# A bidirectional encoder block in float32: common rows for x and the first weights, seven products for SwiGLU's first pair, sums of weights made in DRAM, and a halved last tile

## The chip, the core and the metric

The kernel runs on one core of a Trainium2 chip. The metric is the device time of one execution in microseconds (us), median of several runs. TensorE (PE in the profile) multiplies; VectorE (DVE), ScalarE (ACT) and GpSimd (POOL) do the rest; SyncE (SP), POOL and ACT issue transfers (DMA).

## The reference, cut to what matters

x has 512 tokens of 1024 features; all is float32.

```python
h = rmsnorm(x, g_mix);  proj = h @ w_in            # 1024 x 11264
xc, gb, gc, q, k, v, g_sw, gate_a, gate_r = split(proj)
y_a = (gb * conv3(gc * xc)) @ w_a_out
y_r = (groupnorm(retention(rotary(q), rotary(k), v)) * g_ret * silu(g_sw)) @ w_r_out
x = x + (sigmoid(gate_a) * y_a + sigmoid(gate_r) * y_r) @ w_o
h2 = rmsnorm(x, g_ffn)
x = x + (silu(h2 @ w_ff_gate) * (h2 @ w_ff_up)) @ w_ff_down      # 2816 wide
y = rmsnorm(x, g_final)
```

## The kernel before

**Arithmetic.** Each float32 operand is split into a high part (rounded to fp32r) and a low part (the rest), and each product is three matmuls: high x high, high x low, low x high. `split` (L170 to L180) makes a high part on ScalarE (L173) and a low part on VectorE (L174). Weights are split on the chip too, in units of 128 x 1024.

**Seven products instead of eight.** Most pairs of weight matrices are treated as a 2 x 2 block matrix b11, b12, b21, b22 (for SwiGLU: gate and up are the two block columns, the halves of the features the two block rows), and the activations as a11 ... a22 by halves of tokens and features. Strassen's scheme in Winograd's form needs seven products, with sums of activations (s1 to s4, `sums`, L588) and sums of weights: t1 = b11 + b12, t2 = t1 + b22, t3 = b12 + b22, t4 = t2 + b21. `prefetch_form` (L243) makes a sum of weights in place on VectorE (L251), and then splits it. `prod` (L324) is one product for SwiGLU: 24 matmuls of 256 columns. `prod_tm` (L358) is one for the quads of w_in (v with the swish gate, the two branch gates), for w_a_out and for the down projection: 24 matmuls of 512 columns (18 where n is 3).

**The order.** `plan` (L58) lists all units of weights in the order in which they are used. `take` hands out the next one and calls `prefetch` until AHEAD = 2 units are ready; `prefetch` first calls `load_raws`, which issues loads for units up to LEAD = 4 places ahead on SP's queue, into ten raw buffers. The order of instructions on each engine comes from a scheduler that keeps dependencies and goes mostly by program order.

**The start.** x is loaded transposed, in blocks of 128 features; `prefetch(4, ...)` loads x's blocks 0 to 3 and the first block of weights in turns (256 KB, 256 KB, 256 KB, 256 KB, 512 KB, 512 KB), and splits them in turns. WARM = 8 matmuls of ones run while the first data are on their way.

**The middle.** q and k of three heads; six quads (`do_quad`, L656), whose results are stored to DRAM on POOL's queue through nine 128 x 512 tiles; convolution, retention, output projections. The loop over nb (L963) makes the residual stream's four token blocks; `ev_o` normalises each and `tr_o` transposes it.

**SwiGLU.** Eleven pairs of 256 gate and 256 up columns, in parts of 3, 4 and 4, each part followed by its down projection. The first pair (`first_pair`, L1018) takes eight plain products, two of them before the last `tr_o`. `begin(q)` is a11 x b11, `second(q)` a12 x b21, `pair(q)` the other five. `gated` applies silu and makes the activations' sums for the down projection.

**The end.** The last down projection adds into y in SBUF: `to_y` adds a finished 128 x 512 bank and squares it with a sum per row, `rms` makes the reciprocal root, `put` scales and stores. The last product finishes token blocks 0 and 1 of the second half of the columns.

Of the kernel before, what the change touches and what calls it, by code (L numbers as in the profile page):

```python
# [17 lines left out]
P = 128  # L18
# [23 lines left out]
WARM = 8  # L42
# [15 lines left out]
def plan():  # L58
# [68 lines left out]


def loads():
# [11 lines left out]
LOADS = loads()  # L141


@with_exitstack
def block_kernel(ctx: ExitStack, tc: tile.TileContext, xT, xtok, wpack, wquad, cols, decs, rot, g_ffn, g_final, out):
# [59 lines left out]
    def prefetch_block(pieces, loads, splits, inbig):  # L205
# [4 lines left out]
        per = max(1, pieces // 2)  # L210
        m = QH // per
        for c, (o, n) in enumerate(((0, 512), (512, 512), (QH, QH)) if pieces > 2 else ((0, QH), (QH, QH))):
            if loads:
                loads(c)
            nc.sync.dma_start(st[o // QH][:, o % QH:o % QH + n], wpack[i][:, o:o + n])
        for half in range(2):
            hi, lo = unit(inbig)
            units.append((hi, lo))
            for c in range(per):
                sl = slice(c * m, (c + 1) * m)  # L220

                round = None if made else nc.vector.tensor_copy
                made.append(split(st[half][:, sl], hi[:, sl], lo[:, sl], round=round))
                if splits:
                    splits(half * per + c)
        return units

    raws = {}

# [5 lines left out]
    def load_raws(upto):  # L235
        while loaded[0] < len(LOADS) and LOADS[loaded[0]][0] <= upto:
            _, quad, name, u, n = LOADS[loaded[0]]
            t = rawtile()
            nc.sync.dma_start(t[:, 0:n], wquad[loaded[0]][:, 0:n])
# [3 lines left out]
    def prefetch_form(quad, f, u, nk):  # L243
# [3 lines left out]
        here = {"t1": "b11", "t2": "b11", "t4": "b11", "t3": "b12"}.get(f, f)  # L247
        more = {"t1": "b12", "t2": "b22", "t4": "b21", "t3": "b22"}.get(f)
# [7 lines left out]
    def prefetch(pieces=1, loads=None, splits=None):  # L256
# [5 lines left out]
        load_raws(i + LEAD)  # L262
        if x[0] == "c":
            units = prefetch_block(pieces, loads, splits, x[1] == "w_o" and x[2] == 512 and x[4] == 512)
# [93 lines left out]
    def prod_tm(n, lhs, pss, start, stop=False, evict=None, part=None):  # L358

        w = []  # L360
        for u in part or range(0, n, 2):
# [8 lines left out]
            for tt in range(2):  # L370
                for u0, (wh, wl) in units:
                    for k in range(u0, min(u0 + 2, n)):
                        c = slice((k - u0) * 512, (k - u0 + 1) * 512)
                        xh, xl = lhs(k, slice(tt * P, (tt + 1) * P))
                        for i, (l, r) in enumerate(((xh, wh), (xh, wl), (xl, wh))):
                            nc.tensor.matmul(pss[tt], l, r[:, c], start=start and k == 0 and i == 0,  # L376
                                             stop=stop and k == n - 1 and i == 2, skip_group_check=True)
                if evict:
                    evict(tt)
# [57 lines left out]
    def load_x(k, n=1):  # L437
        nc.sync.dma_start(xs[k // 4][:, k % 4:k % 4 + n, :], xT[:, k:k + n, :])

    def split_x(k):  # L440
        split(xs[k // 4][:, k % 4, :], xu[0][k // 4][:, k % 4, :], xu[1][k // 4][:, k % 4, :],
              gmix[:, k:k + 1])
# [4 lines left out]

    def split_next(k):
        with tc.issue_after(made[0].ins):
            split_x(k)  # L450

    prefetch(4, lambda c: load_x(c, 1 + c // 2), split_next)
    prefetch(2, lambda c: load_x(4 + 2 * c, 2), lambda c: split_two(4 + 2 * c))
# [53 lines left out]
    for k in range(8):  # L507

        with tc.issue_after(made[min(k + 1, 3)].ins):
            ss.add(xs[k // 4][:, k % 4, :])  # L510
# [40 lines left out]
    def store(dst, t):  # L551
        nc.gpsimd.dma_start(dst, t)
# [4 lines left out]
    for h in range(EARLY):  # L557
        pss = [bank() for _ in range(4)]
        for kk in range(8):
# [4 lines left out]
            if (h, kk) == (1, 1):  # L564
# [3 lines left out]
                for k in range(8):  # L568
                    xk = xs[k // 4][:, k % 4, :]
                    nc.vector.scalar_tensor_tensor(out=xk, in0=xk, scalar=gmix[:, k:k + 1], in1=rrow,  # L570
# [85 lines left out]
    def do_quad(left, right, func, func_left=None):  # L656
        def ev_sum(dst, o, f):
            def ev(tt, t):
                if f:
                    nc.scalar.activation(t, t, f)  # L660
                store(dst[:, o + tt, :], t)
            return ev

        def ev21(tt, ps):
            t = t512()
            nc.scalar.activation(t, ps, func_left or AF.Copy)
            store(left[:, 2 + tt, :], t)
# [295 lines left out]
    for nb in range(NB):  # L963
# [6 lines left out]
        hs[nb] = ev_o(nb, [po[half][nb] for half in range(2)])  # L970

# [46 lines left out]
    def first_pair():  # L1018
        w = {}
        g0, u0, g1, u1 = bank(), bank(), bank(), bank()  # L1020
        _, (w["b11"],) = take()
        prod(w["b11"], XF[0, 0], g0, True, False)
        _, (w["b21"],) = take()
        prod(w["b21"], XF[1, 0], g0, False)
        tr_o(NB - 1, hs[NB - 1])
        _, (w["b12"],) = take()
        prod(w["b12"], XF[0, 0], u0, True, False)
        _, (w["b22"],) = take()
        prod(w["b22"], XF[1, 0], u0, False)
        gated(0, 0, g0, u0)  # L1030
# [224 lines left out]
```

## Time and profile before

| | |
|---|---|
| three timed runs | 1031.6, 1033.45, 1033.29 us; median 1033.29 |
| the profiled execution | 1033.17 us; span from first to last instruction 1031.4 |
| TensorE busy | 1021.8 us, 5640 matmuls |
| VectorE, ScalarE, POOL busy | 886.6, 529.5, 114.9 us |
| DMA | 175.06 MB, mean 170 GB/s |

Busy is the share of time with an instruction of the engine in flight. Matmuls overlap one another, so a busy TensorE can still run slower than it could; how far apart matmuls start tells that.

### The profile page before, as it was taken

The page shows a single profiled execution, that of the slowest core. Times are in us where ns is not written, and L with a number is a line of the kernel's source. Part 1 is how long each engine was busy: PE and PEld are TensorE (multiplying, and loading weights), DVE is VectorE, ACT ScalarE, POOL GpSimd, SP SyncE. Part 2 cuts the span into 40 slices and gives each one's busy share as a digit, 9 for nine tenths or more (in the row PEclk, how much of TensorE's full clock was granted, in tenths as well). Part 3 has the DMA queues.
Part 4 walks back from the last instruction along what each step waited for, and adds up shares of the span by engine and source line. Part 5 has one row for each costly group of instructions (what it writes and reads, how often), then busy time and mean ns, then how long its engine had stood idle before and what let it go on. Part 6 is the DMA issues. An engine that isn't in the chain of part 4 may idle for free.

```text
span 1031.4 us, 14797 instructions
## 1 busy us (share of the span) xinstructions
PE 1021.8 (99%) x5640; PEld 892.9 (87%) x5640; DVE 886.6 (86%) x1143; ACT 529.5 (51%) x717; POOL 114.9 (11%) x189
## 2 busy tenths in 40 slices
PE   9999999999999999999999999999999999999997
PEld 7888888888888998888888888889988999899985
DVE  7878898979798988697999988579998899889996
ACT  6546655553656455353533235355555565556553
POOL 0030221121112003202011000000002000110011
PEclk9999999999999999999999999999999999999999
DMA  9524376383746657828267625630319332663322
GB/s 345 188 79 171 127 254 203 136 295 113 234 157 216 255 192 262 322 79 314 66 261 286 223 86 184 222 120 4 103 47 278 106 94 71 193 155 103 123 32 92
DMA packets 49399, 175.06 MB, mean 170 GB/s; under 512 B 6512, under 2 KB 6512, under 8 KB 46000
## 3 DMA queue, kind: packets, MB, share of 16 engines
q1 hardware_dynamic: 35584, 129.26, 36.2%
q0 software_dynamic: 13600, 44.84, 13.5%
q8 instruction: 44, 0.72, 0.3%
q14 instruction: 27, 0.22, 0.1%
q10 hardware_dynamic: 144, 0.03, 0.0%
HBM read 135.56 MB, written 38.54 MB: 169 GB/s over the span
## 4 chain that ended last, share of the span: by engine, by line
PE 96%; DVE 2%; DMA 1%; issue 1%; ACT 0%; POOLq 0%; POOL 0%; SPq 0%
PE bank L376 34%; PE bank L332 27%; PE bank L291 11%; PE bank L292 11%; PE bank L293 11%; DMA raw<-wquad 1%; DVE wlo L174 1%; DMA raw<-wpack 0%; PE bank L945 0%; PE bank L896 0%; DVE xform L174 0%; DVE big L174 0%; DVE big L1147 0%; DVE t L998 0%; DVE t L1014 0%
## 5 line engine op out<-in xcount | busy, mean ns | idle before, releaser
L173 ACT CAST whi<-raw 128x1024 fp32r<-128x1024 f32 (+1 forms) x286 | 292.3, 1034 | 288.3 <-PE bank L376 60.6
L174 DVE TENSOR_TENSOR wlo<-raw,whi 128x1024 fp32r<-128x1024 f32 (+1 forms) x287 | 340.2, 1199 | 82.2 <-ACT whi L173 81.1
L332 PE MATMUL bank<-xform,whi 128*128 128x256 f32 x1440 | 260.3, 283 | 0.0
L332 PEld LDWEIGHTS bank<-xform,whi 128*128 128x128 f32 x1440 | 224.8, 192 | 0.7 <-ACT t L383 0.5
L332 PE MATMUL bank<-xform,wlo 128*128 128x256 f32 x720 | 203.7, 283 | 0.0
L376 PE MATMUL bank<-whi,big 128*128 128x512 f32 x596 | 187.5, 390 | 0.2 <-ACT t L383 0.2
L251 DVE TENSOR_TENSOR raw<-raw 128x1024 f32<-128x1024 f32 (+1 forms) x132 | 156.9, 1202 | 3.0 <-DMA raw<-wquad 1.8
L332 PEld LDWEIGHTS bank<-xform,wlo 128*128 128x128 f32 x720 | 138.2, 192 | 0.0
L376 PEld LDWEIGHTS bank<-whi,big 128*128 128x128 f32 x596 | 111.7, 188 | 24.3 <-ACT t L383 0.6
L376 PE MATMUL bank<-whi,xform 128*128 128x512 f32 x384 | 121.2, 389 | 0.0
L376 PE MATMUL bank<-wlo,big 128*128 128x512 f32 x298 | 116.0, 389 | 0.0
L291 PE MATMUL bank<-big,whi 128*128 128x512 f32 x224 | 87.7, 393 | 0.9 <-DVE whi L173 0.9
L292 PE MATMUL bank<-big,whi 128*128 128x512 f32 x224 | 87.5, 392 | 0.0
L293 PE MATMUL bank<-big,wlo 128*128 128x512 f32 x224 | 87.4, 392 | 0.0
L383 ACT COPY t<-bank 128x512 f32<-128x512 f32 x102 | 59.2, 585 | 52.4 <-PE bank L376 26.3
L376 PEld LDWEIGHTS bank<-whi,xform 128*128 128x128 f32 x384 | 72.1, 188 | 15.0
L376 PE MATMUL bank<-wlo,xform 128*128 128x512 f32 x192 | 74.8, 390 | 0.4 <-DVE wlo L174 0.4
L291 PE MATMUL bank<-whi,big 128*128 128x512 f32 x176 | 68.9, 392 | 0.0
L292 PE MATMUL bank<-wlo,big 128*128 128x512 f32 x176 | 68.5, 389 | 0.0
L293 PE MATMUL bank<-whi,big 128*128 128x512 f32 x176 | 68.1, 390 | 0.0
L376 PEld LDWEIGHTS bank<-wlo,big 128*128 128x128 f32 x298 | 56.0, 188 | 11.5
L291 PEld LDWEIGHTS bank<-big,whi 128*128 128x128 f32 x224 | 42.5, 190 | 9.9 <-ACT big L176 1.2
(175 smaller groups left out, 1373.2 us busy)
## 6 DMA issues: line engine op xcount, KB each, us to landing
raw<-wquad SPq DMA_DIRECT2D x132, 512.0 KB, 4.7
raw<-wpack SPq DMA_DIRECT2D x51, 512.0 KB, 6.3
z<-t POOLq DMA_DIRECT2D x24, 256.0 KB, 5.3
zform<-z POOLq DMA_DIRECT2D x6, 1024.0 KB, 6.1
v<-t POOLq DMA_DIRECT2D x16, 256.0 KB, 5.0
sg<-t POOLq DMA_DIRECT2D x16, 256.0 KB, 3.1
qh<-t POOLq DMA_DIRECT2D x16, 256.0 KB, 2.7
ql<-t POOLq DMA_DIRECT2D x16, 256.0 KB, 2.8
```

Source lines behind the costliest of these rows:

```text
L173: first = (round or nc.scalar.copy)(hi, src)
L174: nc.vector.tensor_tensor(out=lo, in0=src, in1=hi.bitcast(F32), op=ALU.subtract)
L251: nc.vector.tensor_tensor(out=t, in0=t, in1=raws[quad, more, u][:, 0:n], op=ALU.add)
L291: nc.tensor.matmul(ps, lh, rh, start=first, stop=False)
L292: nc.tensor.matmul(ps, lh, rl, start=False, stop=False)
L293: nc.tensor.matmul(ps, ll, rh, start=False, stop=last)
L332: nc.tensor.matmul(o, l[:, c], r[:, k], start=start and s == 0 and k == 0 and i == 0, stop=stop and k == 3 and i == 2, skip_group_check=True)
L376: nc.tensor.matmul(pss[tt], l, r[:, c], start=start and k == 0 and i == 0, stop=stop and k == n - 1 and i == 2, skip_group_check=True)
L383: nc.scalar.copy(t, ps)
```

## The change

Five parts:

1. x's blocks 0 to 3 and the first block of weights lie in common rows (`xw`): four transfers of 512 KB, each with 512 columns of x and 512 of weights, into four raw buffers. x's scaling by the row norm writes to another tile than it reads. WARM is 10.
2. The first pair uses the seven products. `begin` and `second` of pairs 0 and 1 and `begin` of pair 2 come before the first `pair`; `tr_o` of the last token block and `sums` come after `second(0)`. Two calls of `prefetch` are added in the loop over nb.
3. For pairs 0 and 1 the sums of weights are made in DRAM by 16 transfers on POOL's queue (8 copies, 8 that add), one after some of the stores of each quad; the finished forms are loaded as raw units, without L251.
4. In the last product the second token block is done by halves of its columns (2 x 256), and each half is added and squared on its own.
5. The final norm multiplies the gain by sqrt(D) beforehand (ScalarE) instead of dividing the sum of squares by D; the sum of squares is finished on POOL instead of VectorE; one of the last stores is issued by ScalarE.

```diff
-WARM = 8
+WARM = 10
...
-    f(0, "b11", "b21", "b12", "b22")
+    f(0, "b11", "b21")
     f(1, "b11", "b21")
+    f(2, "b11")
     for q0, n in FF_PARTS:
-        for q in range(max(q0, 1), q0 + n):
+        for q in range(q0, q0 + n):
             f(q, *(x for x in FORMS[1:5] if q > 1 or x != "b21"))
-            if q + 1 < NQ:
+            if 1 < q < NQ - 1:
                 f(q + 1, "b11")
             f(q, "t4", "b22")
...
+SUMMED = (("f", 0), ("f", 1))
...
-            need = name if quad == ("f", 0) else NEEDS.get(name)
+            need = name if quad in SUMMED else NEEDS.get(name)
...
-    return out
+    return out + [(len(PLAN), quad, "b12", 0, 4 * WIDTH[quad[0]]) for quad in SUMMED]
...
+    steps = [(quad, f, g, add) for group in (
+        (("t1", "b11", 0), ("t3", "b22", 0)), (("t1", "b12", 1), ("t3", "b12", 1)),
+        (("t2", "t1", 0),), (("t2", "b22", 1),), (("t4", "t2", 0),), (("t4", "b21", 1),))
+        for quad in SUMMED for f, g, add in group]
+
+    def sum_step(behind=None):
+        if steps:
+            quad, f, g, add = steps.pop(0)
+            src = wsum[quad, g] if g[0] == "t" else quarter(quad, g)
+            with tc.issue_after(behind.ins):
+                if add:
+                    nc.gpsimd.dma_start(out=wsum[quad, f], in_=src, accum_op=ALU.add, max_dma_last_dim=4 * CH)
+                else:
+                    nc.gpsimd.dma_start(wsum[quad, f], src)
...
+    for k in range(4):
+        nc.sync.dma_start(xw_sb[k], xw[k])
+    units = [unit(), unit()]
+    for k in range(4):
+        sl = slice(k % 2 * 512, (k % 2 + 1) * 512)
+        hi, lo = units[k // 2]
+        made.append(split(xw_sb[k][:, 512:], hi[:, sl], lo[:, sl], round=None if k else nc.vector.tensor_copy))
+        with tc.issue_after(made[0].ins):
+            split_x(k)
...
-                store(dst[:, o + tt, :], t)
+                last = store(dst[:, o + tt, :], t)
+                if tt and not o:
+                    sum_step(last)
...
             if tt:
                 turn_one()
+                sum_step(last)
...
         hs[nb] = ev_o(nb, [po[half][nb] for half in range(2)])
+        if nb in (1, 3):
+            prefetch()
...
-    first_pair()
+    begin(0)
+    second(0)
+    tr_o(NB - 1, hs[NB - 1])
+    XF.update(sums(xf32[0, 0], xf32[1, 0], xf32[0, 1], xf32[1, 1]))
     begin(1)
     second(1)
+    begin(2)
     for q0, n in FF_PARTS:
-        for q in range(max(q0, 1), q0 + n):
+        for q in range(q0, q0 + n):
             pair(q)
...
+    nc.scalar.activation(gf, gf, AF.Copy, scale=float(math.isqrt(D)))
...
     def rms(nb):
-        ac = acs[nb]
-        nc.vector.scalar_tensor_tensor(out=ac[:, 5:6], in0=ac[:, 1:2], scalar=1.0 / D,
-                                       in1=ac[:, 4:5], op0=ALU.mult, op1=ALU.add)
+        ac, i = acs[nb], done[nb] - 1
+        nc.gpsimd.tensor_scalar(out=ac[:, 5:6], in0=ac[:, i:i + 1], scalar1=ac[:, 4:5], scalar2=None, op0=ALU.add)
         nc.gpsimd.tensor_tensor(out=ac[:, 7:8], in0=ac[:, 5:6], in1=mhalf[:, 0:1], op=ALU.pow)
...
-            nc.sync.dma_start(out[nb * P:(nb + 1) * P, half * 512:(half + 1) * 512], yt)
+            (nc.scalar if (nb, half) == (1, 0) else nc.sync).dma_start(
+                out[nb * P:(nb + 1) * P, half * 512:(half + 1) * 512], yt)
...
-    prod_tm(n, forms["s4"], d, False, True, lambda tt: ev(d[tt], tt, 1))
+    prod_tm(n, forms["s4"], d, False, True, lambda tt, c: ev(d[tt], tt, 1, c), halves=True)
```

## Rows read from the trace of the kernel before

**Rows 1.** The page, busy us by engine, share of the span, instructions.

```profile
PE 1021.8 (99%) x5640; PEld 892.9 (87%) x5640; DVE 886.6 (86%) x1143; ACT 529.5 (51%) x717; POOL 114.9 (11%) x189
```

**Rows 2.** Waits of TensorE: us in total, times, longest.

```profile
PE bank L291 <- DVE whi L173: 0.9, 1, 0.9
```

**Rows 3.** The chain that ended last: start us, us, what.

```profile
699.31 57.86 PE bank L332 x480
```

**Rows 4.** Stretches: busy us (instructions) by engine, granted clock, DMA share, GB/s.

```profile
4.80:5.70 0.90, 0.03 (x1) 0.01 (x1) 0.55 (x2) 0.07 (x1) 0.00 (x0) 1.00 0.83 280
5.70:9.60 3.90, 3.88 (x9) 3.13 (x10) 2.84 (x6) 2.56 (x5) 0.00 (x0) 1.00 0.99 339
9.60:26.40 16.80, 16.80 (x75) 13.88 (x75) 15.06 (x20) 12.34 (x19) 0.00 (x0) 1.00 1.02 403
75.00:325.00 250.00, 249.63 (x1102) 206.31 (x1101) 216.46 (x234) 146.67 (x187) 41.53 (x77) 1.00 0.55 192
655.00:692.30 37.30, 37.30 (x185) 31.02 (x184) 21.42 (x33) 17.95 (x34) 1.64 (x3) 1.00 0.36 119
692.30:780.40 88.10, 88.10 (x653) 83.81 (x651) 81.44 (x103) 49.88 (x73) 3.31 (x3) 1.00 0.25 79
1028.25:1029.50 1.25, 0.00 (x0) 0.00 (x0) 0.00 (x0) 0.00 (x0) 0.00 (x0) 0.50 1.01 380
```

**Rows 5.** Groups of VectorE by form, 692.3 to 780.4: busy us, mean ns.

```profile
L174 DVE TENSOR_TENSOR wlo<-raw,whi 128x1024 fp32r<-128x1024 f32 x23 | 28.0, 1219 | 0.9 <-ACT whi L173 0.6
L251 DVE TENSOR_TENSOR raw<-raw 128x1024 f32<-128x1024 f32 x14 | 16.8, 1219 | 1.9 <-DMA raw<-wquad 1.8
...
L1014 DVE TENSOR_TENSOR t<-t,t 128x256 f32<-128x256 f32 x9 | 3.5, 418 | 0.0
```

**Rows 6.** POOL's queue, 90 to 130 and 764 to 800: packets, MB, share.

```profile
q0 software_dynamic: 960, 3.15, 20.9%
...
q0 software_dynamic: 1147, 2.09, 34.0%
```

**Rows 7.** Waits of SP's queue: us in total, times, longest.

```profile
SPq L239 <- DVE wlo L174: 519.8, 112, 39.9
```

**Rows 8.** Loads of line L239, 75 to 325.

```profile
DMA to landing us min/median/max: 3.4/4.8/7.5
```

**Rows 9.** Timeline of the start: start us, us, instruction, idle before.

```profile
0.73 0.39 SPq L438 DMA_DIRECT2D big<-xT  x1
...
1.05 3.79 PE L424 MATMUL bank<-ones 128*128 128x128 f32 x16 [1.05 <-DVE lw L609]
...
4.15 0.72 ACT L176 ACTIVATE big<-big,cols_sb 128x512 fp32r<-128x512 f32 x1 [1.40 <-DMA cols_sb<-cols]
...
5.15 0.43 DVE L173 CAST whi<-raw 128x512 fp32r<-128x512 f32 x1 [4.14 <-DMA raw<-wpack]
...
5.72 1.62 PE L291 MATMUL bank<-big,whi 128*128 128x512 f32 x3 [0.89 <-DVE whi L173]
```

**Rows 10.** Loads of x, line L438.

```profile
DMA to landing us min/median/max: 3.2/6.2/9.5
```

**Rows 11.** Timeline of the tail.

```profile
1013.03 0.19 POOL L1126 TENSOR_SCALAR fin<-fin 128x1 f32<-128x1 f32 x1 [8.67 <-ACT t L1124]
...
1024.30 0.69 DVE L1122 TENSOR_TENSOR big<-bank,big 128x512 f32<-128x512 f32 x1 [0.64 <-PE bank L376]
...
1025.03 0.63 ACT L1124 ACTIVATE t<-big 128x512 f32<-128x512 f32 x1 [1.99 <-DVE big L1122]
...
1026.02 0.54 POOL L1135 TENSOR_TENSOR fin<-fin,mhalf 128x1 f32<-128x1 f32 x1 [1.74 <-DVE fin L1133]
...
1026.60 0.75 DVE L1147 SCALAR_TENSOR_TENSOR big<-big,fin,gf 128x512 f32<-128x512 f32 x1 [0.66 <-POOL fin L1135]
1027.38 0.81 SPq L1150 DMA_DIRECT2D y<-big  x2
```

**Rows 12.** A 256-column form on ScalarE, 735 to 745.

```profile
L173 ACT CAST big<-t 128x256 fp32r<-128x256 f32 x1 | 0.4, 402 | 0.0
```

More of the change, by code (lines that the diff above doesn't have):

```diff
@@ L1 @@
+import math
 from contextlib import ExitStack
@@ L203, in unit, with prefetch_block @@
         return hi, lo
-    def prefetch_block(pieces, loads, splits, inbig):
+    def prefetch_block(loads, splits, inbig):
         i = block[0]
@@ L209, in prefetch_block, with quarter @@
         units = []
-        per = max(1, pieces // 2)
-        m = QH // per
-        for c, (o, n) in enumerate(((0, 512), (512, 512), (QH, QH)) if pieces > 2 else ((0, QH), (QH, QH))):
+        for c in range(2):
             if loads:
                 loads(c)
-            nc.sync.dma_start(st[o // QH][:, o % QH:o % QH + n], wpack[i][:, o:o + n])
-        for half in range(2):
+            nc.sync.dma_start(st[c], wpack[i][:, c * QH:(c + 1) * QH])
+        for c in range(2):
             hi, lo = unit(inbig)
             units.append((hi, lo))
[L219 to L225, printed above, removed]
+            split(st[c], hi, lo)
+            if splits:
+                splits(c)
         return units
     raws = {}
+    wsum = {(quad, f): dram.tile([P, QH], F32, name=f"{f}{quad[0]}{quad[1]}")
+            for quad in SUMMED for f in ("t1", "t2", "t3", "t4")}
+    def quarter(quad, name, u=0):
+        return wquad[next(i for i, x in enumerate(QUARTERS) if x[1:4] == (quad, name, u))]
+    steps = [(quad, f, g, add) for group in (
[11 more added lines that the diff above has]
+                    nc.gpsimd.dma_start(wsum[quad, f], src)
     def rawtile():
@@ L238, in load_raws @@
             t = rawtile()
-            nc.sync.dma_start(t[:, 0:n], wquad[loaded[0]][:, 0:n])
+            src = wsum[quad, name] if name[0] == "t" else quarter(quad, name, u)
+            nc.sync.dma_start(t[:, 0:n], src[:, 0:n])
             raws[quad, name, u] = t
@@ L246, in prefetch_form @@
         n = nk * WIDTH[quad[0]]
-        here = {"t1": "b11", "t2": "b11", "t4": "b11", "t3": "b12"}.get(f, f)
-        more = {"t1": "b12", "t2": "b22", "t4": "b21", "t3": "b22"}.get(f)
+        if quad in SUMMED:
+            here, more = f, None
+        else:
+            here = {"t1": "b11", "t2": "b11", "t4": "b11", "t3": "b12"}.get(f, f)
+            more = {"t1": "b12", "t2": "b22", "t4": "b21", "t3": "b22"}.get(f)
         t = raws[quad, here, u][:, 0:n]
@@ L254, in prefetch_form, with prefetch @@
         return [(hi, lo)]
-    def prefetch(pieces=1, loads=None, splits=None):
+    def prefetch(first=False, loads=None, splits=None):
         i = pos[0]
@@ L261, in prefetch @@
         x = PLAN[i]
-        load_raws(i + LEAD)
+        if not first:
+            load_raws(i + LEAD)
         if x[0] == "c":
-            units = prefetch_block(pieces, loads, splits, x[1] == "w_o" and x[2] == 512 and x[4] == 512)
+            units = prefetch_block(loads, splits, x[1] == "w_o" and x[2] == 512 and x[4] == 512)
         else:
@@ L356, in fm_quad, with prod_tm @@
         ev12(u2)
-    def prod_tm(n, lhs, pss, start, stop=False, evict=None, part=None):
+    def prod_tm(n, lhs, pss, start, stop=False, evict=None, part=None, halves=False):
         w = []
@@ L446, in split_two @@
         split_x(k + 1)
[L448 to L453, printed above, removed]
+    prefetch(True, lambda c: load_x(4 + 2 * c), lambda c: split_two(4 + 2 * c))
     rcs = misctile(D, "rcs").rearrange("p (i n) -> p i n", i=2)
@@ L509, in block_kernel @@
         with tc.issue_after(made[min(k + 1, 3)].ins):
-            ss.add(xs[k // 4][:, k % 4, :])
+            ss.add(x_in(k))
     ss.split()
@@ L1172, in block_kernel, with ev @@
     held = []
-    def ev(ps, nb, half):
-        add, square = to_y(ps, nb, half)
+    def ev(ps, nb, half, c):
+        add, square = to_y(ps, nb, half, c)
         if held:
```

104 lines of the change are left out of this document (50 added, 54 removed).

## Prediction

> **What bounds the kernel now.** I read the page first: TensorE is busy 99% of the span [rows 1]. A busy row need not mean full speed, so the waits of TensorE came next: the longest wait of a real matmul is the first one, 0.9 us for the first rounded weights [rows 2]. The chain of waits says at what pace it then runs: 480 matmuls of 256 columns in 57.86 us, 120.5 ns each, one behind the other [rows 3]; the table by stretches gives 75 matmuls of 512 columns in 16.8 us, 224 ns each [rows 4]. So from 5.72 to 1024.3 the time is a count of matmuls, and a change is worth what it does to that count, to the start and to the tail. VectorE is the runner-up: 81.44 of 88.10 us busy in the stretch of the first SwiGLU pairs [rows 4].
>
> The sum is made against the profiled execution: 1033.17 us, span 1031.4 and 1.8 around it. The median of the three timed runs is 1033.29, 0.12 higher; they lie between 1031.6 and 1033.45.
>
> **The change, part by part.**
>
> *One product fewer.* The first pair takes seven products in place of eight. A product is 24 matmuls of 256 columns: 24 x 0.1205 = 2.89 us off the count [rows 3]. This is the surest term, -2.89.
>
> *What feeds it.* The stretch 692.3 to 780.4 holds the first pairs and the start of the first down product. There VectorE loses four sums of weights of pair 1 (4 x 1.22 = 4.88, L251), gains three more splits for pair 0 (3 x 1.22 = 3.66) and three evictions that pair 0 did not have (its b, u3 and u2; 3 x 0.69 = 2.07), and two splits (2.44) move forward by the two added prefetch calls, to 655 to 692.3, where it is busy 21.42 of 37.30 us [rows 4, 5]. That makes 81.44 - 1.59 = 79.85 us of work for a stretch of 88.10 - 2.89 = 85.2 us: 94% instead of 92%. It fits if nothing waits at a bad place. The tightest place is pair 0's s1 and s2: the four sums of activations follow the last transposes as before, but only three products (8.7 us) stand between those and the first use, where eight stood. From the ends far apart (0 if the splits hide, 3.7 us below in the rivals) I take +0.5, near zero, because TensorE's row stays at 88.10 of 88.10 today with VectorE at 92%.
>
> *The sums in DRAM.* Sixteen transfers of 512 KB go on POOL's queue during the six quads: eight copies, eight that add. Nothing on TensorE's path reads them before the first pairs, 300 us later. Price from the queue view: plain stores took 20.9% of 40 us for 3.15 MB, 1.39 us per 512 KB; adding stores 34.0% of 36 us for 2.09 MB, 3.07 us per 512 KB [rows 6]. Together 8 x 1.39 + 8 x 3.07 = 35.7 us of all sixteen DMA engines, over 250 us in which they are 0.55 busy [rows 4]. What hides them: weight loads are sent as soon as a raw buffer is free (SP waited 519.8 us for that, over 112 loads) and land in 4.8 us [rows 7, 8]. I take 0 and keep 35.7 as the far end. Behind each on POOL stand the next stores of the quads, and VectorE and ScalarE wait for the tiles that these free. Pairs 0 and 1 now load seven forms each instead of four blocks; with the DMA engines 0.25 busy there [rows 4], 0. After the last weights two blocks (b12 of both pairs) are loaded that nobody reads: 2 x 1.39 us, some 20 us before SP's last stores; 0.
>
> *The start.* Today x's first block and the first weights are two transfers; the first block alone lands 3.2 us after its issue at 0.73, and the weights let VectorE begin at 5.15 [rows 9, 10]. One transfer of both, issued at 0.73, lands between 3.9 and 5.1; I take 4.6. Then comes ScalarE's 0.72 on x beside VectorE's 0.43 on the weights [rows 9], so data are ready near 5.4. The warm-up grows from 16 rows in 3.79 us to 20, to about 5.8 by the rows' ends, somewhat less by their starts. First real matmul 5.3 to 5.8 instead of 5.72: I take -0.2. Four of the ten raw buffers now hold x until 35 us; the loads that must wait are those that ran far ahead; 0.
>
> *The clock.* In 5.7 to 9.6 nine matmuls took 3.9 us, 433 ns each; from 9.6 on, 224 [rows 4]. That is the spacing of 512 columns at 1.2 and at 2.4 GHz (the column of the granted clock reads 1.00 in both, so here the spacing is what shows it). Before the rise TensorE stood idle 0.9 us between warm-up and first matmul [rows 4]. The longer warm-up closes that gap nearly. What is lost at the lower level is 9 x 0.209 = 1.9 us: the gain lies between 0 (the rise comes at 9.6 as before) and 1.9. I take 1.2: the fastest of the three runs is 1.7 us below the median, about the size of this loss, so executions that lose almost none of it seem to exist. The Trainium skill, TensorE: Matmul & The Clock Gate, "What's actually happening", says that the slow clock is the default and activity releases it; by that rule closing the gap brings the rise forward, and the sum would have 1.9 here, 1028.5 in all (the second rival). Its section "What you observe" calls the moment variable from run to run; no row of this one execution shows that.
>
> *The tail.* From the last add at 1024.30 the chain is: square 0.73 later, rstd by POOL at 1026.02, scale at 1026.60, first store at 1027.38, both stores issued by 1028.19, end at 1031.4 [rows 11]. Now the last half tile is 256 columns: VectorE's 0.69 becomes 0.42 and ScalarE's 0.63 becomes 0.40 [rows 5, 11, 12], 0.50 off. But in the last 2.89 us VectorE has 0.69 + 1.41 + 0.42 + 0.75 = 3.3 us to do (adds and scalings of the tiles before), so the last add starts up to 0.4 late. The sum of squares moves from VectorE to a POOL TENSOR_SCALAR of 0.19 [rows 11]; about nothing. I take -0.3 of 0 to -0.5. Sending one of the two last stores from ScalarE saves half of 0.81 us of issue, 0.4 at most (nothing stands behind it on ScalarE); but while both move, the DMA engines are at 1.01 and 380 GB/s [rows 4], so I take -0.1. The Trainium skill, DMA: Bandwidth & Descriptors, "Issuing engines are not separate DMA queues", says that a second issuing engine saves the issue time only; by that rule the term would be up to -0.4 and the sum 1028.9, by the row of the full engines it is -0.1. The halved matmuls cost 24 x 0.1205 - 12 x 0.224 = +0.20. Tail: -0.2.
>
> *The rest* (gain times sqrt(D) on ScalarE, which is half idle; x's scaling into another tile): 0.
>
> Sum: -2.89 + 0.5 - 0.2 - 1.2 - 0.2 = -4.0. 1033.17 - 4.0 = 1029.2 us.
>
> **The rivals.**
>
> *The clock does not move.* The start brings at most its 0.2, partly spent at the lower level: 1029.2 + 1.2 = 1030.4. For it: nothing in the rows says what the rise asks for; 16 rows of warm-up did not bring it before 9.6. Against: the idle gap was there. Here the change does not do what its longer warm-up would.
>
> *The clock rises with the first real matmul.* All of the 1.9 comes back: 1029.2 - 0.7 = 1028.5. For it: the gap is nearly closed, and the fastest run before. Against: 0.1 to 0.4 us of idle time may stay, and the data of the next blocks must then arrive for 2.7 us (12 x 0.224) each, which 512 KB in 1.4 us do, but VectorE has three operations of 0.69 to 0.75 on each, 2.2 in all.
>
> *VectorE becomes the bound in the first pairs.* If its 6.66 us of idle time in the stretch (88.10 - 81.44) cannot be filled, the stretch takes 79.85 + 6.66 = 86.5 instead of 85.2, and 1.3 comes back; if the two splits are not made early either, 82.3 + 6.66 = 88.95, and 3.7 comes back. Without the 0.5 already counted: 1030.0 to 1032.4, middle 1031.5. For it: 92% busy today. Against: no wait of TensorE there that counts.
>
> *The DRAM sums hold up the stores (slower).* Stores share POOL's queue with the sums. One that lands late keeps its 512-column tile (nine in all); VectorE, in order, stops before the next weight split, and TensorE has only two prepared units of 2.7 us (12 x 0.224). If all of it passed on, 1029.2 + 35.7 = 1064.9. Forecast gains are used up when 11% passes (4.0 of 35.7); it is slower by 0.2% from 17% (6.1); a quarter gives 1038. For it: VectorE 87% busy in 75 to 325 [rows 4] with stores in every quad. Against: each sum is some 3.1 us, and a quad, seven products of 24 matmuls of 0.224, lasts 37.6 and has three.
>
> **How the numbers follow.** A measurement here tells about 0.2% (2.07 us) from no change. Forecast (gap closed, one product fewer, little lost): 0.50, own range 1028.0 to 1030.2. Clock as before: 0.20. Clock up at once: 0.09. VectorE bound: 0.13; its middle, 1031.5, lies within 0.2% of before (above 1031.2). DRAM sums: 0.08. Faster: 0.50 + 0.20 + 0.09 = 0.79; same 0.13; slower 0.08. The range leaves out the DRAM rival, the far end of VectorE's and small tails of the others: 1027.8 to 1031.8.
>
> **What would show it.** Right: matmuls of L332's kind 24 fewer; the first pairs without a wait of TensorE over 0.5 us; the first real matmul near 5.5 and spacings of 224 ns before 9; the adding transfers near 3 us of queue time each and no wait on a store in VectorE's list; the last add 0.42 long. Wrong: a wait of TensorE on an s1 or s2 split near 705, on weight splits in 75 to 325, or 433 ns until 9.6 again. The prediction falls if TensorE's idle time grows by over 2 us anywhere.

## The result

The changed kernel takes 1034.19 us (median of 22 runs, 1032.8 to 1036.36) where the kernel before takes 1032.7 (22 runs, 1031.12 to 1034.77): ratio 1.0016, 95% interval 1.001 to 1.0022. It is slower by 0.16%, within 0.2% of no change; 1029.2 had been forecast, and the range ended at 1031.8. The profiled execution took 1034.5 us, its span is 1032.7, against 1033.17 and 1031.4.

The page of the changed kernel: busy us by engine, share, instructions.

```profile
PE 1020.1 (99%) x5632; PEld 890.8 (86%) x5632; DVE 886.1 (86%) x1142; ACT 536.1 (52%) x726; POOL 125.6 (12%) x210
```

Against [rows 1] TensorE has eight matmuls fewer (24 of the saved product; plus 12 by halving, plus 4 of warm-up) and still the longer span. Where it stands is in its waits, without that of the warm-up: us in total, times, longest.

```profile
...
PE bank L408 <- DVE big L1160: 1.0, 1, 1.0
PE bank L363 <- DVE xform L184: 1.0, 1, 1.0
PE bank L363 <- ACT whi L183: 0.8, 1, 0.8
PE bank L363 <- ACT t L416: 0.5, 1, 0.5
PE bank L322 <- ACT big L186: 0.4, 1, 0.4
PE bank L408 <- DVE big L184: 0.4, 1, 0.4
PE bank L323 <- DMA big<-ql: 0.3, 1, 0.3
```

The kernel before had one wait of 0.9 us that counted [rows 2]. Now L1160, the first line, is the add of a finished bank in the last tile; the three of L363 are in the first SwiGLU pairs; L322 is the first real matmul. The wait on L184 in L363 is the sign that the prediction had named, a wait on a split of s2. The stretches of [rows 4], with the same columns:

```profile
5.70:9.60 3.90, 3.48 (x13) 2.90 (x14) 3.75 (x7) 3.50 (x7) 0.00 (x0) 1.00 1.01 369
...
75.00:325.00 250.00, 250.00 (x1109) 207.16 (x1108) 216.40 (x235) 146.10 (x185) 52.24 (x92) 1.00 0.69 224
655.00:692.30 37.30, 37.30 (x185) 31.07 (x184) 22.42 (x36) 18.21 (x36) 1.64 (x3) 1.00 0.35 121
692.30:780.40 88.10, 85.82 (x623) 80.60 (x622) 81.16 (x103) 54.89 (x78) 2.36 (x3) 1.00 0.34 115
```

Thirteen matmuls lie in the first stretch instead of nine, although the first starts 0.40 us later. The quads, where the sums in DRAM are made (75 to 325), keep TensorE busy all the time. In the first pairs (692.3 to 780.4) it stands idle for 2.28 us.

With matmuls of both kernels laid side by side by their place in the order, the 1.30 us of longer span are: first matmul +0.40; the next ten -1.37; at 82 us -0.70 (a stall of the kernel before is missing); at 520 us +0.63 (the wait for ql); up to the first pairs -0.06; in them -2.89 for the product and +3.53 of waits; from 760 to 785 us -0.34; at 872 us +0.66; last tile and end +1.44.

### The profile page after: what moved, and what is told of

The parts are those of the page before. It is cut to its first block, busy times and chain, and to the rows that moved or that the text cites. A ratio compares the mean times of both kernels' runs of the same rounds, so it can differ in the third digit from the quotient of the medians.

```text
span 1032.7 us, 14838 instructions
## 1 busy us (share of the span) xinstructions
PE 1020.1 (99%) x5632; PEld 890.8 (86%) x5632; DVE 886.1 (86%) x1142; ACT 536.1 (52%) x726; POOL 125.6 (12%) x210
## 4 chain that ended last, share of the span: by engine, by line
PE 68%; issue 17%; DVE 8%; POOL 3%; DMA 2%; ACT 1%; POOLq 0%; SPq 0%; DVEq 0%; ACTq 0%
PE bank L408 31%; PE bank L363 16%; PE bank L322 7%; PE bank L323 7%; PE bank L324 7%; DVE wlo L184 2%; POOL z L597 2%; DVE big L198 1%; DMA big<-ql 1%; DVE big L184 1%; DVE raw L281 1%; DMA z<-t 1%; DMA raw<-wquad 0%; DMA cols_sb<-cols 0%; ACT whi L183 0%
## 5 line engine op out<-in xcount | busy, mean ns | idle before, releaser
L184 DVE TENSOR_TENSOR wlo<-raw,whi 128x1024 fp32r<-128x1024 f32 (+1 forms) x290 | 343.4, 1199 | 87.8 <-ACT whi L183 86.6
L363 PE MATMUL bank<-xform,whi 128*128 128x256 f32 x1424 | 258.2, 284 | 2.3 <-DVE xform L184 1.0
L363 PEld LDWEIGHTS bank<-xform,whi 128*128 128x128 f32 x1424 | 222.2, 192 | 3.9 <-ACT t L416 1.6
L363 PE MATMUL bank<-xform,wlo 128*128 128x256 f32 x712 | 200.8, 283 | 0.0
L408 PE MATMUL bank<-whi,big 128*128 128x512 f32 (+1 forms) x604 | 188.0, 387 | 1.4 <-DVE big L1160 1.0
L281 DVE TENSOR_TENSOR raw<-raw 128x1024 f32<-128x1024 f32 x128 | 152.2, 1202 | 1.7 <-DMA raw<-wquad 0.6
L363 PEld LDWEIGHTS bank<-xform,wlo 128*128 128x128 f32 x712 | 136.3, 192 | 0.0
L408 PE MATMUL bank<-wlo,big 128*128 128x512 f32 (+1 forms) x302 | 116.6, 387 | 0.0
L322 PE MATMUL bank<-big,whi 128*128 128x512 f32 x224 | 87.3, 392 | 0.4 <-ACT big L186 0.4
L322 PE MATMUL bank<-whi,big 128*128 128x512 f32 x176 | 68.9, 392 | 0.0
L323 PE MATMUL bank<-wlo,big 128*128 128x512 f32 x176 | 68.6, 390 | 0.0
L324 PE MATMUL bank<-whi,big 128*128 128x512 f32 x176 | 68.1, 390 | 0.0
L322 PEld LDWEIGHTS bank<-big,whi 128*128 128x128 f32 x224 | 42.3, 189 | 9.4 <-ACT big L186 0.7
```

The costliest lines, as they stand in the source:

```text
L184: nc.vector.tensor_tensor(out=lo, in0=src, in1=hi.bitcast(F32), op=ALU.subtract)
L281: nc.vector.tensor_tensor(out=t, in0=t, in1=raws[quad, more, u][:, 0:n], op=ALU.add)
L322: nc.tensor.matmul(ps, lh, rh, start=first, stop=False)
L323: nc.tensor.matmul(ps, lh, rl, start=False, stop=False)
L324: nc.tensor.matmul(ps, ll, rh, start=False, stop=last)
L363: nc.tensor.matmul(o, l[:, c], r[:, k], start=start and s == 0 and k == 0 and i == 0, stop=stop and k == 3 and i == 2, skip_group_check=True)
```

## The experiments

Each ran in alternation with the kernel before, eleven times or so; ratios are to it, with the 95% interval.

| run | us | ratio |
|---|---|---|
| changed kernel again (c_after) | 1034.05 | 1.0013 (1.0004 to 1.0022) |
| e1_whole | 1032.55 | 0.9998 (0.9989 to 1.0006) |
| e2_two_banks | 1033.12 | 1.0006 (0.9997 to 1.0015) |
| e13_store_sp | 1032.02 | 0.9996 (0.9987 to 1.0005) |
| e7_tail_back | 1031.95 | 0.9993 (0.9984 to 1.0002) |
| e3_sums_first | 1033.68 | 1.0009 (1.0 to 1.0018) |
| e8_pool_s4 | 1034.3 | 1.0014 (1.0005 to 1.0023) |
| e12_order_only | 1034.38 | 1.0019 (1.001 to 1.0028) |
| e6_pe_order | 1031.99 | 0.999 (0.9982 to 0.9999) |
| e4_cols_first | 1033.56 | 1.0011 (1.0002 to 1.0019) |
| e11_before_warm10 | 1031.9 | 0.9996 (0.9988 to 1.0005) |
| e10_no_dram_sums | 1032.12 | 0.9996 (0.9987 to 1.0005) |
| e9_best | 1029.77 | 0.9978 (0.9969 to 0.9987) |

### The last tile and the end

The timeline of the changed kernel's last tile: start us, us, instruction, idle before and its releaser.

```profile
1022.04 1.41 DVE L1186 SCALAR_TENSOR_TENSOR big<-big,fin,gf 128x512 f32<-128x512 f32 x2
...
1022.54 0.28 PE L408 MATMUL bank<-whi,big 128*128 128x256 f32 x1
...
1023.36 0.42 DVE L1160 TENSOR_TENSOR big<-bank,big 128x256 f32<-128x256 f32 x1
...
1023.83 0.39 PE L408 MATMUL bank<-whi,big 128*128 128x256 f32 x1 [1.01 <-DVE big L1160]
...
1027.66 0.75 DVE L1186 SCALAR_TENSOR_TENSOR big<-big,fin,gf 128x512 f32<-128x512 f32 x1 [1.68 <-POOL fin L1174]
```

The first half's last matmul ends at 1022.82. VectorE is at two scalings until 1023.4, adds that half, and only then, 1.29 us after the last start, TensorE begins the second half: other columns, but the same bank. The wait is one for a semaphore that this add raises. Two runs take the wait away in two ways.

```diff
-    prod_tm(n, forms["s4"], d, False, True, lambda tt, c: ev(d[tt], tt, 1, c), halves=True)
+    prod_tm(n, forms["s4"], d, False, True, lambda tt, c: ev(d[tt], tt, 1, c))          # e1_whole
```

> The changed kernel with its last tile whole again (twelve matmuls of 512 columns and one add of 0.69 us, in place of twice twelve of 256 and two adds of 0.42); all else as changed. Theory A (the halves share one PSUM bank; TensorE may not write the second half while VectorE has still to add the first, and VectorE comes to that add late because two scalings of 1.41 us stand before it): the 1.29 us gap at 1022.5 and the 0.17 us that halving costs go, the last add and square are 0.27 and 0.22 longer, so the end is 0.9 to 1.3 us earlier than in the changed kernel, that is 0.3 to 0.7 above the kernel before. Rival B (VectorE is simply behind in the tail, and the gap of TensorE only shows it): the last add stays where it is or later, 0 to 0.4 us gained, 1.2 to 1.6 above before.

```diff
+    d[1] = (d[1], bank())                              # e2_two_banks: columns 256 to 511 in the second
-    prod_tm(n, forms["s1"], d, True)
+    prod_tm(n, forms["s1"], d, True, halves=True)
...
+lambda tt, c: ev(d[1][c.start // 256] if tt else d[0], tt, 1, c), halves=True)
```

> The changed kernel with the last tile's two halves in two PSUM banks (its first product s1 is halved as well, so 12 more matmuls of 512 become 24 of 256, +0.17 us; its add of the tile before becomes two of 256). Theory A (it is the shared bank): the gap of 1.29 us at the start of the last half goes, last add about 1.2 us earlier, net 0.9 to 1.2 us below the changed kernel, 0.4 to 0.7 above before. Rival B (VectorE is behind anyway): the gap goes, but the last add starts less than 0.5 us earlier; 0 to 0.3 gained. Rival C (the wait is not on the bank but on VectorE's queue in some other way): the gap stays.

In both the gap is gone: the spacings from 1015 on are 0.09 and 0.07 us above normal in sum, against 1.33. The timeline with two banks:

```profile
1022.53 0.40 PE L412 MATMUL bank<-whi,big 128*128 128x256 f32 x2
1022.77 0.28 PE L412 MATMUL bank<-wlo,big 128*128 128x256 f32 x1
...
1023.97 0.28 PE L412 MATMUL bank<-whi,big 128*128 128x256 f32 x1
...
1024.28 0.75 DVE L1197 SCALAR_TENSOR_TENSOR big<-big,fin,gf 128x512 f32<-128x512 f32 x1 [0.52 <-POOL fin L1185]
1024.95 0.42 DVE L1164 TENSOR_TENSOR big<-bank,big 128x256 f32<-128x256 f32 x1
```

So the shared bank is the cause of the gap. From the start of the two scalings to the end of the span it is 10.69 us in the changed kernel and 9.70 in e1: 0.99 gained, theory A's size. In e2 it is 10.08. Of the 1.2 us gained there on TensorE only part reaches the end: the last add now waits for a scaling that stands ahead of it on VectorE (1024.28), and from last matmul to ScalarE's last read it is 1.75 us instead of 1.10. In e2 theory A was right on the wait and half of its size; rival B had the other half. The Trainium skill, PSUM — Partial Sum Buffer, "PSUM bank collisions raise a hardware error", says that two engines must not be in one bank (and the same 32 partitions of it) at a time, disjoint columns included, and that programs should guard a bank by semaphores. The trace has such an order (1.29 us from start to start in one bank, 0.12 in two); no run shows what would happen without it.

```diff
-        nc.gpsimd.tensor_scalar(out=ac[:, 5:6], in0=ac[:, i:i + 1], scalar1=ac[:, 4:5], ...)
+        nc.vector.tensor_scalar(out=ac[:, 5:6], in0=ac[:, i:i + 1], scalar1=ac[:, 4:5], ...)   # e7 only
-            (nc.scalar if (nb, half) == (1, 0) else nc.sync).dma_start(
+            nc.sync.dma_start(                                                      # e7 and e13, both with e1
```

> The changed kernel with its whole tail as before: last tile whole, the sum of the two sums of squares on VectorE, all last stores on SP's queue (the gain times the root of D on ScalarE stays). Theory A (three costs: shared bank about 1.2, POOL's sum 0.28 to 0.4, ScalarE's store 0.2): 1.5 to 1.9 us less than the changed kernel, 0.5 to 0.9 less than the run with the whole last tile alone; from ScalarE's read of the last sum of squares to the last scaling 0.85 us, from that to the end 4.8. Rival B (POOL's sum and the store are within the noise of a profile): as the run with the whole last tile alone, within 0.3.

> The changed kernel with its last tile whole and all last stores on SP's queue; the sum of the two sums of squares stays on POOL. Theory A (the store from ScalarE costs some 0.5 us: from the last scaling to the end 5.04 and 5.09 us with it, 4.45 and 4.52 without it in the kernels with the tail as before): last scaling to end 4.4 to 4.6, 0.4 to 0.6 us less than the run with the whole last tile alone. Rival B (what saved it there was VectorE's sum, and the order of the two last scalings): last scaling to end stays at 5.0 or more.

From the end of ScalarE's last read to the last scaling, and from the start of that to the end of the span: before 0.84 and 4.80; changed 1.13 and 5.07; e1 1.08 and 5.07; e13 1.07 and 4.49; e7 0.91 and 4.47. POOL's sum costs 0.2 to 0.3, ScalarE's store 0.6 against the same kernel without it (theory A of e13); e7 is near theory A's 0.85 and beats its 4.8. By the medians it is 2.10 us below the changed kernel (c_after), where its theory A had 1.5 to 1.9. The transfers in the last 20 us, KB each and us to landing, changed kernel and then e13:

```profile
y<-big SPq DMA_DIRECT2D x7, 256.0 KB, 2.1
y<-big ACTq DMA_DIRECT2D x1, 256.0 KB, 2.8
```

```profile
y<-big SPq DMA_DIRECT2D x8, 256.0 KB, 2.0
```

The last landing comes 3.58 us after the last scaling in e1 and 3.48 in e13, so the transfer itself is 0.1 of the 0.6. The rest lies behind the last landing: 1.49 us to the end in e1, 1.00 in e13. There SP waits for the semaphores of the last transfers one after another, in a fixed order; then it drains, and the engines meet. In the kernels with a store from ScalarE SP also pauses for some 0.3 us among these steps; why is open.

The same stretch tells why the kernel before, with both stores on SP as well, needs 4.80 (4.80 to 4.81 in four further profiles). Its last store raises a semaphore that stands early in that order: seven more waits of 0.06 us follow the landing at 1030.07, and SP first drains 0.51 us after it. In e13 one more wait follows the landing at 1028.99, and the drain comes 0.16 us after it. SP's drains in the kernel before, then in e13 (ns, first and last start):

```profile
L1251 SPq DRAIN  x3: 7/7/7, 1030.6 to 1030.9; - x3
```

```profile
L1300 SPq DRAIN  x3: 7/7/7, 1029.1 to 1029.5; - x3
```

### The first pairs

The changed kernel at pair 0's s2 and s3:

```profile
709.56 0.28 PE L363 MATMUL bank<-xform,whi 128*128 128x256 f32 x1
709.58 1.22 DVE L184 TENSOR_TENSOR xform<-big,xform 128x1024 fp32r<-128x1024 f32 x1
...
710.85 0.39 PE L363 MATMUL bank<-xform,whi 128*128 128x256 f32 x1 [1.00 <-DVE xform L184]
...
713.78 1.05 ACT L183 CAST whi<-raw 128x1024 fp32r<-128x1024 f32 x1 [2.10 <-PE bank L363]
...
714.88 0.38 PE L363 MATMUL bank<-xform,whi 128*128 128x256 f32 x1 [0.78 <-ACT whi L183]
...
724.23 1.23 DVE L184 TENSOR_TENSOR wlo<-raw,whi 128x1024 fp32r<-128x1024 f32 x1 [2.86 <-ACT whi L183]
```

TensorE has issued one matmul of s2's high part when the low part is only begun: VectorE, which has no idle time from 695.2 on, is 1.1 us late. The second wait is for a cast that itself waited 2.10 us for TensorE to release a weight buffer: on TensorE some matmuls of pair 1's s1 and s2 stand ahead of pair 0's s3. At 724 VectorE is idle for 2.86 us, so over the whole pair it is not the bound.

```diff
-                ("s1", a22, a21, a22, ...), ("s3", a21, a11, a21, ...),
-                ("s2", a11, a22, a11, ...), ("s4", a12, a12, a11, ...)
+                ("s1", a22, a21, a22, ...), ("s2", a22, a22, a11, ...),     # e3 and e8, second set only
+                ("s3", a21, a11, a21, ...), ("s4", a12, a12, a22, ...)
-            nc.vector.tensor_tensor(out=o, in0=in0, in1=in1, op=op)
+            (nc.gpsimd if s2_next and name == "s4" else nc.vector).tensor_tensor(...)          # e8 only
...
```

(e8 also queues ScalarE's casts of pair 0's weights for s1 and s2 behind its casts of the sums.)

> The changed kernel, with the second set of sums of activations made in the order s1, s2, s3, s4 (s2 overwrites s1's sum, not a11), in place of s1, s3, s2, s4; same operations. Theory A (the stalls of the first pairs come from the order: s2's low part is made by VectorE at 709.6 to 710.8, behind s3's sum and split, 1.0 us after TensorE wants it): s2 is ready 2.4 us or more earlier, the gap at 709.6 (1.16 us above a normal spacing) goes, the kernel gains 0.9 to 1.2 us. Rival B (VectorE is the bound of the stretch; work put off only stalls TensorE later): the gap at 709.6 goes, others of the same sum (at s3, s4 or at the weights of pair 1) take its place, gain below 0.3 us.

> The changed kernel with the second set of sums in the order s1, s2, s3, s4, its s4 sum (128 x 1024, 1.22 us on VectorE) made by POOL, and ScalarE's casts of the weights for pair 0 queued behind the casts of the sums. Theory A (VectorE has no idle time from 695 to 719 and is the bound there; the order alone changed nothing, the same gaps came back to a hundredth): with 1.22 us less to do before s2's low part the gap of 1.28 us at 709.6 goes or falls below 0.3, 0.9 to 1.2 us gained, if POOL's add does not slow VectorE. Rival B (the gap is ScalarE's or TensorE's order, not VectorE's load): gap as before, or moved to s3 with the same sum; nothing gained.

In e3 the same gaps stand at the same distance, 1.28 and 1.06 us. Neither of its theories was met, because the edit did not bring the split forward: ScalarE casts s2 only at 706.95, behind a cast of weights that waits 1.83 us for TensorE to release a buffer, and VectorE takes the split up at 708.80 as before. In e8 the gaps are 1.22 and 1.52, and the reason is new:

```profile
705.68 2.87 POOL L642 TENSOR_TENSOR big<-big 128x1024 f32<-128x1024 f32 x1 [11.58 <-DVE big L642]
...
706.28 5.63 DVE L184 TENSOR_TENSOR xform<-big,xform 128x1024 fp32r<-128x1024 f32 x3
```

The three splits that take 3.49 us in e3 (at 708.80) take 5.63 beside POOL's add: 1.22 us were taken off VectorE and 2.14 put on it. The Trainium skill, SBUF — State Buffer, "Who interferes with whom", says that a VectorE tensor_tensor with both inputs in SBUF contends with POOL's reads; this pair of rows agrees. The run therefore does not tell load from order.

```diff
+        with tc.issue_after(heads_of[0]["s3"].ins) if q == 1 else nullcontext():     # e6 and e12
             _, (w,) = take()
             prod(w, XF["s1"], d, True)
             _, (w,) = take()
             prod(w, XF["s2"], a, False)
         u2 = snap(a)
-        if q > 1:
-            second(q)
+        if q == 0 or q > 2:                                                           # e6 only
+            second(q or 2)
+        elif q == 2:
+            begin(3)
...
```

> The changed kernel with TensorE's order in the first pairs changed: pair 1's first two products are queued behind pair 0's s3 product (in the changed kernel two matmuls of each stand ahead of it), the second product of pair 2's p1 stands between pair 0's s2 and s3, and pair 3's first product between pair 2's s2 and s3. Same products, same work of VectorE. Theory A (the gap of 1.06 us at 713.8 is one of order: a matmul of pair 1 that waits for a weight cast, itself waiting for a weight buffer, stands ahead of pair 0's ready product): that gap goes, 0.6 to 0.9 us gained. Rival B (VectorE has no time left from 695 to 719, and what TensorE does not wait for here it waits for later): the sum of the gaps from 700 to 745 stays at 2.7 us or more, within 0.4.

> The changed kernel with only the order of the matmuls kept: pair 1's first two products behind pair 0's s3 product, without the products of pairs 2 and 3 as cover. Theory A (cover is what was missing: at 709.6 VectorE is 1.1 us late with s2's low part, and TensorE has no product that needs neither that nor the copy of the bank): the gap at 709.6 stays at 1.1 to 1.3, the one at 713.8 becomes a wait of 0.6 to 1.0 for the copy of the bank; 0 to 0.4 us gained. Rival B (the order by itself made the gaps): both gaps go, 1.7 to 2.1 us gained, as with the cover.

(In e6 the list of weights follows the new order.) These two tell it apart. With the order alone (e12) the gap at 708.4 stays at 1.28 and the next grows to 1.78, more than theory A had for it; nothing is gained. The wait is now for the copy of the bank, 1.5 us of the 2.0:

```profile
PE bank L364 <- ACT t L418: 2.0, 2, 1.5
```

With a product of pair 2 as cover (e6) both gaps are gone, though VectorE does the same work as late as before. Between the first matmul of s2's high part (708.64) and the first that waits for its low part (709.93), TensorE now starts nine matmuls of another product (708.76 to 709.73). Sum of spacings above normal from 700 to 736: before 0.34, changed 3.83, e12 4.30, e6 1.48. The longest waits of e6:

```profile
...
PE bank L413 <- DVE big L1168: 1.0, 1, 1.0
PE bank L326 <- DMA big<-ql: 0.5, 1, 0.5
PE bank L367 <- ACT t L421: 0.5, 1, 0.5
...
```

L367 (L363 in the changed kernel) keeps only the wait for pair 1's copy. What was missing was a product that needs neither s2 nor the copied bank, at the moment when VectorE was late. e6 is 2.06 us below the changed kernel in the same series; its theory A had only one of the two gaps going, for 0.6 to 0.9. Cover without the new order was not run.

### The start and the clock

c_after is the changed kernel with no edit; e4 has one line changed; e11 is the kernel before with one.

```diff
-    nc.scalar.dma_start(cols_sb, cols)
+    nc.sync.dma_start(cols_sb, cols)          # e4_cols_first
...
-WARM = 8
+WARM = 10                                     # e11_before_warm10, in the kernel before
```

> The changed kernel again, unchanged, as the measure for the other three on the same chip. Both theories: 1.0 to 2.3 us above the kernel before. Of the start, theory A (the first run's late first matmul, 6.13, was one execution's late landing of the columns) says 5.4 here, as in three of the four runs since; rival B (the common rows make it late) says 6.0 or later.

> The changed kernel with the 28 KB of columns (g_mix among them) issued as the first transfer of SP's queue, ahead of the common rows of x and weights, not on ScalarE's queue beside them. Theory A (ScalarE's first split of x waits for the columns, which share the DMA engines with four transfers of 512 KB and land 4.6 us after their issue): the columns land by about 4.0, the first split of x starts when the first common row lands (4.6 to 5.2), the first real matmul comes 0.3 to 0.6 us earlier than 6.13, and the end with it. Rival B (the row is no earlier than the columns, and is now issued later): the first real matmul at 6.0 to 6.3, nothing gained.

> The kernel before with the warm-up of ten products in place of eight, nothing else. Theory A (the longer warm-up alone brings the full clock to the first real matmuls: a run of the changed kernel with the first real matmul at 5.96, after a gap of 1.24 us, has 0.23 us per 512 columns at once): first real matmul at 5.7 to 5.8, spacing 0.23 from the first or third on in place of 0.43 up to 9.6; 1.3 to 1.9 us less than the kernel before. Rival B (what counts is the gap between warm-up and first matmul, or the earlier data of the common rows): the spacing stays at 0.43 for eight or nine matmuls, nothing gained.

The first real matmul starts at 6.12 us in the first profile of the changed kernel, at 5.49 in c_after, and at 5.29 to 5.50 in the ten others that have its start. In the first one ScalarE waited for the columns until 5.35, in c_after until 4.71. But the first common row was as late there: VectorE began on its weights at 5.16, in c_after at 4.53. In e4 the columns land 1.7 us after their issue, but the first common row comes later (5.12), and the matmul is at 5.96: rival B, nothing gained.

In e11 the spacing is 0.23 us from the third matmul on, as theory A said. It gained 0.7 us by the medians, less than A's 1.3 and not told from nothing by the interval. Part of the difference is in e11 itself, whose profile loses 0.4 us at 520 us and 0.4 at 872 where the four profiles of the kernel before lose next to nothing. The larger part shows when the kernel before is profiled three times more, with no edit.

> The kernel before, unchanged, for another profile of its start. Its times lie in two groups, near 1031.4 and near 1033.4; the profile shown belongs to the upper one. Theory A (the groups are the first matmuls at the lower level or not): an execution near 1031.4 shows 0.23 us per 512 columns from the second or third matmul on, one near 1033.4 0.43 up to 9.6. Rival B (the groups have another cause): spacing of 0.43 in both.

> As the run above, a second look. Theory A: spacing 0.23 us from the second or third matmul on if its time is near 1031.4, 0.43 up to 9.6 if it is near 1033.4. Rival B: the same spacing whatever its time.

> As the run above, a third look. Theory A: spacing 0.23 us from the second or third matmul on if its time is near 1031.4, 0.43 up to 9.6 if it is near 1033.4. Rival B: the same spacing whatever its time.

The three executions took 1031.17, 1033.18 and 1031.4 us. TensorE alone in the stretch of [rows 4], first the one of 1031.17, then that of 1033.18, then e11: busy us, matmuls, granted clock.

```profile
5.70:9.60 3.90, 3.73 (x16) 1.00 1.02 382
```

```profile
5.70:9.60 3.90, 3.83 (x9) 1.00 1.02 336
```

```profile
5.70:9.60 3.90, 3.89 (x16) 1.00 1.01 347
```

Sixteen matmuls or nine in the same time: spacings of 0.23 us, that of 512 columns at 2.4 GHz, or 0.43, that of 1.2. The third execution has 16 too. From the start of the last warm-up matmul to the first real one it is 1.47 and 1.35 us in the two with 16, 1.37 in the one with nine, so this gap is not what decides. The granted clock reads 1.00 in all three rows because a trace has no record of it ahead of its first one. That first record, of the full clock, begins at 4.75 and 5.18 us in the two executions with 16 and at 10.61 in the one with nine; in the first profile of the kernel before it begins at 9.56, in e11 at 6.50. Each time the spacing is wide up to that moment and 0.23 behind it.

With a warm-up of ten every profile here (14) has the short spacing from the third matmul on at the latest, and the full clock from between 4.11 and 7.05 us; with eight, two of four. The times of the kernel before lie in two groups, near 1031.4 and near 1033.4 (56 of 137 below 1032.4, 81 above); all twelve of e11 are below 1032.3. In the four profiles the groups are this: theory A.

### The sums in DRAM, and the two cures together

e9 is e6 and e7 in one kernel; e10 is e9 with one line more:

```diff
-SUMMED = (("f", 0), ("f", 1))
+SUMMED = ()
```

> The two edits that helped together: TensorE's order in the first pairs with a product of pair 2 as cover, and the whole tail as before (last tile whole, sum of squares on VectorE, stores from SP). Theory A (the two losses are separate, 2.1 us each against the changed kernel in the same runs): 1029.5 to 1030.3 us, 0.2 to 0.35% below the kernel before and below every kernel so far. Rival B (the gains overlap, because the later stages wait for the same transfers anyway): 1031 or more.

> The kernel with both edits, with no sums of weights in DRAM: pairs 0 and 1 load the four blocks each and VectorE makes their eight sums (1.22 us each). Theory A (the DRAM sums cost nothing where they are made, and take 9.8 us from VectorE where it has no idle time): gaps of TensorE of 3 us or more come back in the first pairs (VectorE has some 5 us of idle time up to 730), so 2 to 6 us slower than with them. Rival B (VectorE's load in the first pairs does not decide, the cover by ready products does, and the DRAM sums cost as much in the quads as they bring): within 0.7 us of the kernel with them.

e9 takes 1029.77 us: 0.22% below the kernel before, and below all others. The two losses were separate (theory A). Its waits from the first real matmul on are two:

```profile
PE bank L367 <- ACT t L421: 0.5, 1, 0.5
PE bank L413 <- DVE big L187: 0.4, 1, 0.4
```

Without the sums in DRAM, e10 is 2.35 us slower. Up to 515 us its matmuls stand 0.28 ahead of those of e9 by its start, and stay there through all the quads: making the sums costs nothing there. At 520 us it has a wait for ql that e9 has not (0.66), and from 705 to 785 it loses 2.03, in several waits of 0.3 to 0.9, among them

```profile
PE bank L367 <- ACT t L421: 1.4, 3, 0.7
```

Theory A, at the lower end: 9.8 us more work of VectorE became 2.0 of TensorE.

## Why the prediction was wrong

The terms, as they were forecast and as the two profiled executions differ:

| term | forecast | measured |
|---|---|---|
| one product fewer | -2.89 | -2.89 |
| waits in the first pairs | +0.5 | +3.53 |
| sums in DRAM | 0 | 0 (e10) |
| start | -0.2 | +0.40; -0.2 to -0.4 in eleven other profiles |
| clock | -1.2 | -1.37 |
| tail | -0.2 | +1.44 |
| elsewhere | 0 | +0.19 (-0.70, +0.63, -0.06, -0.34, +0.66) |
| sum | -4.0 | +1.30 |

**What feeds the product** is the step that cost most. It named the place (s1 and s2, three products of cover where eight stood) and then sized it by the share of busy time, 94% of a stretch of 85 us. But VectorE is full from 695 to 719 and idle for 2.86 us before 724; what counts is whether a product is ready at the moment when it is late. The +0.5 was 3.53. The rival in which VectorE becomes the bound had about this size (3.7) by another mechanism: e6 removed 2.35 of it with VectorE's work untouched. That VectorE's load still counts, e10 shows: 9.8 us more of it cost 2.0.

**The tail** is the second. Its own terms on the chain were near: the shorter add and square gave 0.59 instead of 0.50, and the halved matmuls cost 0.17 instead of 0.20. Missing was that add and matmuls of two halves share a bank: +1.27 on TensorE with its restart. "About nothing" for POOL's sum was 0.29. The second issuer's -0.1 was +0.27 against the kernel before, and +0.58 against the same tail without it.

**The clock** was sized rightly against the profiled execution (-1.37 for -1.2), in part by luck: the full clock came at 7.05 us in this execution of the changed kernel, later than in all 13 other profiles with the longer warm-up. And the profiled execution belonged to the slower group of the kernel before. The faster group (56 of 137) had no such loss to give back; e11, the longer warm-up alone, is worth 0.7 by the medians. The prediction saw that the fastest run lay 1.7 us lower and drew from it only that the gain was possible.

**The start** was right but for the one execution in which the first row and the columns landed some 0.6 us late; **the sums in DRAM** were right, and the slower rival built on them did not happen. The forecast's own test, idle time of TensorE grown by over 2 us, was met in 692.3 to 780.4 (2.28). The -0.70 at 82 us and the +0.63 at 520 come and go between executions of one kernel; the second stands in ten of the 13 profiles of changed kernels and in none of the four of the kernel before. The +0.66 at 872, a wait for a split at the start of the second down projection, stands in all changed kernels (+0.4 to +1.2) and, with +0.4, in e11; no run took it away, and its cause is open. One slip in the working: the middle of 1030.0 to 1032.4, the rival in which VectorE becomes the bound, is 1031.2 and not 1031.5.

## What to carry to other kernels

A saved product is worth its matmuls only if, wherever a helper engine is late, another product is ready that needs nothing of it: look for that at the moment of use, in the order of TensorE, not in the mean of busy time. Splitting the last tile to shorten the tail needed a PSUM bank for each part here, and for its whole gain the last adds on VectorE must not stand behind other work. A saving at the start should be held against several executions: if the times before lie in two groups, the profile shows only one of them.

## What was not expected of the hardware

- Matmuls to columns 256 to 511 of a bank waited, by a semaphore, for VectorE's read of columns 0 to 255: 1.29 us from start to start, 0.12 in two banks.
- POOL's add of 128 x 1024 (2.87 us) stretched three VectorE splits beside it from 3.49 to 5.63 us.
- The same kernel starts with 0.23 or with 0.43 us between its first matmuls of 512 columns (executions of 1031.17 and 1033.18 us); the first record of the full clock begins at 4.75 us in the one and at 10.61 in the other.
- With one of the two last stores on ScalarE's queue it is 5.07 us from the last scaling to the end, with both on SP's 4.49; the last landing is only 0.1 later (3.58 and 3.48).
- In the kernel before, 0.51 us pass between the last landing and SP's first drain, in e13 0.16: the order in which SP waits for semaphores that are already raised.
